# A planned two-layer decoder trunk: half-array products grouped, look-ahead limits per stage, norm weights loaded at first use, large buffers in sets of 18 and 6

## The chip, the cores and the metric

The kernel runs on one core of one Trainium2 chip. The metric is the device time of one execution in microseconds (us), smaller being better. The profile names the engines of the core: PE (TensorE; matrix products, and PEld for its weight loads), DVE (VectorE), ACT (ScalarE), POOL (GpSimd) and SP (SyncE, whose instructions start the DMA transfers).

## The reference

Two layers act on x of 512 positions by 1024 features, in float32. Cut to what matters here:

```python
for i in range(2):
    h = rmsnorm(x, mix_pre_g[i])
    z = h @ w_in[i]                       # 1024 -> 3206 columns, split among three mixers
    out_a = gelu(a_u) * (causal(sgu_w) @ rmsnorm(gelu(a_v)) + sgu_b)   # 4 groups x 64, chunks of 128
    out_b = silu(r_g) * rmsnorm(retention(rotary(r_q), rotary(r_k), r_v))   # 6 heads x 64, chunkwise
    out_c = softmax(f_q @ f_k.T / 8 + c_i - c_j, causal) @ f_v         # 6 heads x 64, c = cumsum(log_sigmoid(f_f))
    x = x + rmsnorm(concat(out_a, out_b, out_c) @ w_o[i], mix_post_g[i])

    h = rmsnorm(x, ffn_pre_g[i])
    g = causal_dwconv3(h @ w_gate[i])     # 1024 -> 4096
    x = x + rmsnorm((gelu(g) * (h @ w_up[i])) @ w_down[i], ffn_post_g[i])

    gate = sigmoid(rmsnorm(x, ple_pre_g[i]) @ w_ple_gate[i])
    x = x + rmsnorm((p[i] @ w_ple_proj[i]) * gate, ple_post_g[i])
```

## The kernel before

**How the work is tiled.** Activations lie with features on the 128 partitions (`hT`, `cc`), four chunks of 128 positions side by side. The large products don't run in plain float32: each operand is split into a high and a low part of the type float32r (`split`, L587: a copy on ACT, a subtraction on DVE), and a product is three float32r products (high by high, high by low, low by high; `mm3`). The names to know are `thl` and `fhl` (split weights), `traw`, `fraw` and `graw` (weights as they come from DRAM), `hT` and `cc` (split activations), `wg`, `wsa`, `wsb` and `wu` (the weights of an FFN block), and `gain` (the weight vectors of the norm before and of the norm after, broadcast over the partitions).

**Half-array products.** Attention and retention run in plain float32, two heads of 64 at a time, and most of their products use 64 rows or 64 columns of the array: in `fox_attend` (L904) the scores `sps` (64 rows, one product for each of two heads and each chunk `c`, of 128, 256, 384 and 512 columns) and the outputs `ops` (64 columns, eight products); in `ret_core` (L959) `ips`, `kvps` and `rops`; in `gating` (L810) four full products, also named `sps`; in `fox_values` (L849) four `cumps`. In the profile a plain float32 product has two records, a float32r product one. A page of the profile that says x14 for `ops` thus speaks of seven products.

**The stages of a layer**, with the stretches of the profiled execution for the first and the second layer: the start (0 to 54, with the first norm and the gating projection); projections and mixers (`mixers`, L777; 54 to 230, and 850 to 1026); the output projection, the embedding product and the entry to the FFN (`out_proj`, L1044; `embed`, L1224; `Seven`, L640, which makes the seven operands of a fast matrix product; 230 to 340, and 1026 to 1135); the steady FFN (`gate_up`, L1082, 32 blocks, with the pieces of `down`, L1133, between them; 340 to 740, and 1135 to 1535); the end of the FFN and the per-layer-embedding gate (`ple`, L1239; 740 to 850, and 1535 to 1612.5).

In `mixers` the three pairs of attention heads are p0, p1 and p2, and so are those of retention. Each attention pair takes scores (`sps`), a softmax on DVE and ACT (`pe`), transposes on PE (`tps`), and outputs (`ops`). Each retention pair ends with `rops`, an ACT square, a DVE sum, two POOL instructions (`vh`, and `y`, a power), a DVE product (`ro`) and transposes on PE (`cps`). Meanwhile PE can run the projections `rps`, `fps` and `gps` (24 float32r products for a block of 128 columns), and later the output projection `wo`.

**What sets the order.** The whole program is first recorded (`record`, L150: every instruction with its dependencies, its buffers and an estimated cost) and then put in order by a planner (`issue`, L224). It simulates the five engines and always gives a free engine the ready instruction that was recorded first. The order that comes out is fixed for each engine (L410), so an instruction that waits holds up all behind it on its engine. Since all instructions are issued from one place, the profile puts all of them on line 408, and groups are told apart by their tiles.

An instruction that opens a new buffer may be taken ahead of the program's order, but `blocked` (L265) holds it back when the buffer's first use lies more than `AHEAD` = 350 recorded instructions ahead of the oldest unfinished one, or when the buffers in between would run short. There are 24 large buffers of 8 KB per partition in two sets (`SETS`, L59): 15 in set X for float32r tiles, 9 in set W for the FFN block's `wg`, `wsa`, `wsb`; other large tiles (kind None in `b8`, L509) go to whichever set has room. There are 12 work buffers of 512 columns (`wk`) and 8 PSUM banks.

The function `gains` (L542) makes the tile `gain` and starts its two DMAs where it is called in the main loop (L1294 to L1301), ahead of the sub-layer that uses it.

```python
if not slots[tag] or s - front > self.AHEAD or (s > front and live[tag][front:s].max() >= bufs):
    return queue(t)
```

Of the kernel before, what the change touches and what calls it, by code (L numbers as in the profile page):

```python
# [27 lines left out]
F32 = mybir.dt.float32  # L28
# [21 lines left out]
class Plan:  # L50
# [8 lines left out]
    SETS = {"X": 15, "W": 9}  # L59

    AHEAD = 350
# [3 lines left out]
    TABLES = (AF.Exp, AF.Gelu_apprx_tanh, AF.Silu, AF.Sigmoid, AF.Sin)  # L65
    HOP = {"PE": 197, "DVE": 128, "ACT": 131, "POOL": 80, "SP": 0}
    HOP_PE = {"PE": 0, "DVE": 250, "ACT": 270, "POOL": 190, "SP": 100}

    def __init__(self, tc):
# [5 lines left out]
        self.fenced = self.strict = False  # L75
        self.kind = {}
# [73 lines left out]
    def record(self, engine, fn, method, args, kw):  # L150
# [23 lines left out]
        if engine == "PE":  # L174
# [6 lines left out]
            t[6:] = [i]  # L181
        self.ops.append((engine, fn, args, kw, deps, used, self.cost(engine, method, outs, ins, args, kw)))

    def cost(self, engine, method, outs, ins, args, kw):
# [13 lines left out]
        if engine == "PE":  # L198
            if method == "transpose":
                return 108, 0, n  # L200
            dt, rows = kw["lhsT"].dtype, kw["lhsT"].shape[0] / P
            if dt == F32R:
                return 0.4427 * n, 0, n * rows
            half = 0.5 if kw["lhsT"].shape[0] == 64 or kw["lhsT"].shape[-1] == 64 else 1
            return half * max(222, n * 4 / 2.4 + 4) if dt == F32 else max(56, n / 2.4), 0, (2 if dt == F32 else 1) * n * rows
        if engine == "ACT":
            func = ([v for v in args if isinstance(v, AF)] + [None])[0]
            self.table[len(self.ops)] = func if func in self.TABLES else None
            pointers += method == "mul" and isinstance(args[2], bass.AP)
            return (50 if psum else 97) + n / 1.196 + 93 * pointers + 93 * ("accum_out" in kw), 0  # L210
# [11 lines left out]
        return 68 + 62 * bool(pointers) + n / rate, 0  # L222

    def issue(self):  # L224
# [35 lines left out]
        order = []  # L260
        parked = {tag: [] for tag in (*slots, *(f"b8 {k}" for k in (*self.SETS, None)))}
# [3 lines left out]
        def blocked(i):  # L265


            for t in ops[i][5]:
# [93 lines left out]
        while len(order) < n:  # L362
            progress = False
            for e in names:
# [117 lines left out]
def body(ctx, tc, a, out):  # L482
# [59 lines left out]
    def gains(post, pre):  # L542

        t = b8("gain", (2, D))
        for i, src in enumerate((post, pre)):
            if src is not None:
                name, l = src
                SY.dma_start(out=t[:, i, :], in_=a[name][l:l + 1, :].to_broadcast([P, D]))
        return t
# [783 lines left out]
```

## Time and profile before

| What | Value |
|---|---|
| time, median of 3 runs | 1617.17 us (1614.98 to 1617.46) |
| the profiled execution's own time | 1614.3 us |
| its span | 1612.5 us |
| granted TensorE clock over the span | 0.998 |
| DVE, ACT, POOL busy | 77%, 52%, 6% |
| bytes moved by DMA | 197.49 MB, 122 GB/s on average |

The span is the time from the first to the last instruction that the profiler records; the execution's own time has some 2 us around it. In the views quoted below, a row of the timeline gives start, duration, engine, operation, output and inputs, and the count of records that it sums up; in brackets stands how long the engine had been idle before it, and what it waited for. Records overlap at their ends, so the distance from one start to the next is the cost of a group, not its duration. A row of the view of windows gives busy times of PE, PEld, DVE, ACT and POOL in a stretch, then the granted clock, the DMA share and GB/s.

### The profile page before, as it was taken

Reading aid. Unit: us, or ns where it says so; the run is one execution under the profiler, and the core shown is the slowest. Engines: PE = TensorE matmul, PEld = TensorE weight load, DVE = VectorE, ACT = ScalarE, POOL = GpSimd, SP = SyncE. Lnnn points to the kernel's source line nnn. Section 1 sums busy time; section 2 is a strip of 40 time slices with the busy share of each in tenths; the row PEclk is TensorE's granted clock in tenths of the full one; section 3 lists DMA queues with packets and bytes.
Section 4 is the critical chain, followed back from the end, with each engine's and each line's share of the span. In section 5 each row is a group of like instructions: output and inputs, shape, how many; then the busy total and the mean of one; then the engine's idle time right before and its main releaser. Section 6 shows DMA issues by size and latency. Waiting matters only on the chain. (4 is left out here: it accounts for less than half of the span.)

```text
span 1612.5 us, 25222 instructions
## 1 busy us (share of the span) xinstructions
PE 1577.5 (98%) x10034; PEld 1393.0 (86%) x10034; DVE 1240.0 (77%) x2013; ACT 840.5 (52%) x1380; POOL 92.0 (6%) x157
## 2 busy tenths in 40 slices
PE   8999998999999999999999999999999999999998
PEld 6887777999999999998888777789999999999977
DVE  6556759988889889877664658599888888888684
ACT  7335526765555555554552445377555455455452
POOL 1000021000000000002220000200000000000022
PEclk9999999999999999999999999999999999999999
DMA  8231316323423423337534114072233233233551
GB/s 298 89 123 53 126 60 222 131 79 105 128 83 105 130 80 105 131 101 270 180 121 157 53 53 170 29 248 92 80 130 105 81 129 105 85 128 107 185 189 53
DMA packets 63422, 197.49 MB, mean 122 GB/s; under 512 B 7348, under 2 KB 15164, under 8 KB 63304
## 3 DMA queue, kind: packets, MB, share of 16 engines
q1 hardware_dynamic: 63160, 195.81, 35.5%
q8 instruction: 79, 1.29, 0.3%
q14 instruction: 39, 0.32, 0.1%
q10 hardware_dynamic: 144, 0.07, 0.0%
HBM read 178.52 MB, written 17.33 MB: 121 GB/s over the span
## 5 line engine op out<-in xcount | busy, mean ns | idle before, releaser
L408 PE MATMUL dn<-thl,act 128*128 128x512 f32 x1536 | 371.5, 391 | 0.0
L408 PEld LDWEIGHTS dn<-thl,act 128*128 128x128 f32 x1536 | 280.0, 188 | 51.9
L408 PE MATMUL ps<-thl,hT 128*128 128x512 f32 (+3 forms) x984 | 207.6, 369 | 1.8 <-DVE thl L408 1.7
L408 PEld LDWEIGHTS ps<-thl,hT 128*128 128x128 f32 x984 | 177.4, 190 | 24.8 <-DVE thl L408 2.6
L408 DVE TENSOR_TENSOR graw<-graw 128x512 f32<-128x512 f32 x256 | 176.3, 690 | 2.7
L408 DVE TENSOR_TENSOR thl<-traw,thl 128x1024 fp32r<-128x1024 f32 (+2 forms) x120 | 140.8, 1186 | 11.3 <-ACT thl L408 11.0
L408 ACT CAST thl<-traw 128x1024 fp32r<-128x1024 f32 (+2 forms) x120 | 119.5, 1020 | 40.3 <-PE dn L408 27.6
L408 PEld LDWEIGHTS beta<-hb,wg 128*128 128x128 f32 x768 | 97.4, 189 | 9.0 <-DVE wg L408 4.0
L408 PEld LDWEIGHTS beta<-hh,wu 128*128 128x128 f32 x768 | 98.3, 189 | 6.1 <-DVE us L408 1.9
L408 PE MATMUL beta<-hb,wg 128*128 128x256 f32 x768 | 99.8, 278 | 3.6 <-DVE wg L408 3.6
L408 PE MATMUL beta<-hh,wu 128*128 128x256 f32 x768 | 100.7, 281 | 1.5 <-DVE us L408 1.5
L408 PE MATMUL ag<-hb,wg 128*128 128x256 f32 x768 | 100.4, 278 | 0.0
L408 DVE TENSOR_TENSOR wg<-graw,wg 128x1024 fp32r<-128x1024 f32 x64 | 78.3, 1224 | 28.0 <-PE beta L408 17.7
L408 PE MATMUL beta<-hh,wsa 128*128 128x256 f32 x768 | 98.2, 277 | 1.7 <-ACT wsa L408 1.6
L408 DVE TENSOR_TENSOR wsb<-graw,wsb 128x1024 fp32r<-128x1024 f32 x64 | 78.3, 1224 | 27.2 <-PE beta L408 18.2
L408 PE MATMUL ag<-hd,wsa 128*128 128x256 f32 x768 | 98.6, 277 | 0.5 <-DVE gs L408 0.3
L408 DVE SCALAR_TENSOR_TENSOR cv<-gs,cw,cv 128x511 f32<-128x511 f32 (+1 forms) x128 | 95.7, 748 | 3.7 <-ACT cv L408 3.5
L408 PE MATMUL beta<-hh,wsb 128*128 128x256 f32 x768 | 98.2, 277 | 0.0
L408 PE MATMUL ag<-hb,wsb 128*128 128x256 f32 x768 | 97.7, 276 | 0.0
L408 PEld LDWEIGHTS ag<-hb,wg 128*128 128x128 f32 x768 | 94.1, 190 | 0.3
L408 PEld LDWEIGHTS beta<-hh,wsa 128*128 128x128 f32 x768 | 92.2, 188 | 2.2 <-ACT wsa L408 2.1
L408 PEld LDWEIGHTS ag<-hd,wsa 128*128 128x128 f32 x768 | 92.1, 188 | 1.1 <-DVE gs L408 0.9
(193 smaller groups left out, 2609.7 us busy)
## 6 DMA issues: line engine op xcount, KB each, us to landing
graw<-in_w_gu_dram SPq DMA_DIRECT2D x128, 512.0 KB, 5.1
traw<-in_w_dn_dram SPq DMA_DIRECT2D x64, 512.0 KB, 4.9
x<-x SPq DMA_DIRECT2D x40, 512.0 KB, 2.6
fraw<-in_w_fm_dram SPq DMA_DIRECT2D x30, 512.0 KB, 7.6
traw<-in_w_wo_dram SPq DMA_DIRECT2D x16, 512.0 KB, 4.6
traw<-in_w_pg_dram SPq DMA_DIRECT2D x16, 512.0 KB, 10.3
x<-in_x_dram SPq DMA_DIRECT2D x8, 512.0 KB, 6.1
traw<-in_w_uv_dram SPq DMA_DIRECT2D x8, 512.0 KB, 6.6
```

Source lines behind the costliest of these rows:

```text
L408: made = o[1](*[self.map(v) for v in o[2]], **{k: self.map(v) for k, v in o[3].items()})
```

## The change

No instruction of work is added or taken away; instructions are put in another order, and buffers are given out by other rules.

- `plan.together()` marks a group of PE instructions. The first of the group takes over the dependencies and the buffers of all, and the planner issues the rest right behind it (`follows`, `then`). Groups are: the four `sps` of `gating`, the four `cumps`, the two heads' `sps` of each chunk, the eight `ops` of a head pair, the eight `ips`, the six `kvps`, and the eleven `rops`.
- `AHEAD` becomes a table with a limit for each stage. `plan.stage` is set where a stage's code is recorded, and `blocked` counts all the buffers that an instruction needs together.
- The class `Gains` takes the place of `gains`: the tile is made and its DMAs are started where a norm first reads it.
- The 24 large buffers are split 18 to 6 instead of 15 to 9.
- The planner's estimated costs change: a cost of switching between kinds of PE products (`SWITCH`, and 95 into plain float32), more for DVE with `accum_out`, for POOL's power and small instructions, and for ACT on under 64 partitions.

```diff
-    SETS = {"X": 15, "W": 9}
-    AHEAD = 350
+    SETS = {"X": 18, "W": 6}
+    AHEAD = {"mix": 460, "wo": 230, "wo2": 230, "emb": 185, "gu0": 720, "gu": 460, "dn": 245, "end": 770, "pg": 450, "pg2": 120}
+    SWITCH = {"F": 110, "T": 9}
...
+    @contextmanager
+    def together(self):
+        self.group = []
+        yield
+        first, *rest = group = self.group
+        self.group = None
+        for i, j in zip(group, rest):
+            self.ops[j][4].add(i)
+            self.follows[i] = j
+        for j in rest:
+            self.ops[first][4].update(d for d in self.ops[j][4] if d not in group)
+            self.ops[first][5].extend(self.ops[j][5])
...
             if kw.get("op") == ALU.pow:
-                return 300 + 165 * n, 0
-            return 160 if pointers == 0 else 200 + 64 * pointers, 0
+                return 460 + 165 * n, 0
+            return 300, 0
...
-                    if not slots[tag] or s - front > self.AHEAD or (s > front and live[tag][front:s].max() >= bufs):
+                    need[tag] += 1
+                    if len(slots[tag]) < need[tag] or s - front > self.AHEAD[self.stages[i]] or (s > front and live[tag][front:s].max() + need[tag] > bufs):
                         return queue(t)
...
-                    _, i = heapq.heappop(ready[e])
+                    if e == "PE" and then is not None:
+                        i = then
+                        ready[e].remove((i, i))
+                        heapq.heapify(ready[e])
+                    else:
+                        _, i = heapq.heappop(ready[e])
...
-    def gains(post, pre):
-        t = b8("gain", (2, D))
-        for i, src in enumerate((post, pre)):
...
+    class Gains:
+        def __init__(self, post, pre):
+            self.src, self.t = (post, pre), None
+        def __getitem__(self, at):
+            if self.t is None:
+                self.t = b8("gain", (2, D))
...
-                for ps, fs in zip(pss, heads):
-                    T.matmul(ps[:, 0:n], lhsT=q[fs, c * P:n], rhs=k[fs, 0:n], start=True, stop=True)
+                with plan.together():
+                    for ps, fs in zip(pss, heads):
+                        T.matmul(ps[:, 0:n], lhsT=q[fs, c * P:n], rhs=k[fs, 0:n], start=True, stop=True)
```

Three places show how PE's order moves. In these rows xN counts instructions, and the number behind a name tells apart the tiles of one name.

The first is the outputs of the first layer's attention pair p1, in PE's order, about 131 to 142 us in the profile of before. Before:

```order
L408 MATMUL rps<-hT,fhl 128x512 x8
L408 MATMUL ops<-fet,mix_414 64x512
L408 MATMUL rps<-hT,fhl 128x512 x10
L408 MATMUL tps<-k_ident,pe 128x128 x4
L408 MATMUL rps<-hT,fhl 128x512 x5
L408 MATMUL ops<-fet,mix_414 64x512
L408 MATMUL ops<-fet,mix_414 64x384 x2
L408 MATMUL ops<-fet,mix_414 64x256 x2
L408 MATMUL ops<-fet,mix_414 64x128 x2
```

And in the changed kernel, at the same place:

```order
L444 MATMUL tps<-k_ident,pe 128x128 x4
L444 MATMUL rps<-hT,fhl 128x512 x8
L444 MATMUL ops<-fet,mix_413 64x512 x2
L444 MATMUL ops<-fet,mix_413 64x384 x2
L444 MATMUL ops<-fet,mix_413 64x256 x2
L444 MATMUL ops<-fet,mix_413 64x128 x2
L444 MATMUL rps<-hT,fhl 128x512 x23
```

The first `ops` product, which stood alone among the projection's products, has moved down to the other seven.

The second is the end of the first layer's retention, on PE: `rops` of p1, then products of the output projection (`wo`, one name for four PSUM banks), then the transposes `cps` that wait for ACT, DVE and POOL. Before:

```order
L408 MATMUL rops<-mix_184,inn 128x64 x4
L408 MATMUL wo_1776<-thl,cc 128x512 x2
L408 MATMUL wo_1819<-thl,cc 128x512 x3
L408 MATMUL wo_1758<-thl,cc 128x512 x3
L408 MATMUL wo_1776<-thl,cc 128x512 x3
L408 MATMUL wo_1819<-thl,cc 128x512 x3
L408 MATMUL wo_1758<-thl,cc 128x512 x3
L408 MATMUL wo_1776<-thl,cc 128x512 x2
L408 MATMUL cps<-k_ident,ro 128x128 x4
```

And in the changed kernel:

```order
L444 MATMUL rops<-mix_171,inn 128x64 x2
L444 MATMUL wo_1762<-thl,cc 128x512
L444 MATMUL wo_1768<-thl,cc 128x512 x3
L444 MATMUL wo_1785<-thl,cc 128x512 x3
L444 MATMUL wo_1793<-thl,cc 128x512 x3
L444 MATMUL wo_1762<-thl,cc 128x512 x3
L444 MATMUL wo_1768<-thl,cc 128x512 x3
L444 MATMUL wo_1785<-thl,cc 128x512 x3
L444 MATMUL wo_1793<-thl,cc 128x512 x3
L444 MATMUL wo_1762<-thl,cc 128x512 x3
L444 MATMUL wo_1768<-thl,cc 128x512
L444 MATMUL cps<-k_ident,ro 128x128 x4
```

Between `rops` and `cps` there are now 26 products where 19 stood. For p2, a little later, 22 products and four transposes stand where 20 products stood; all four banks of `wo` are now open.

The third is the end of the second layer's FFN on PE: the last pieces of `down` (`dn`), the transposes `hps` of the next norm's operand, and the first products of the gate (`ps<-thl,hT`). Before:

```order
L408 MATMUL hps<-k_ident,h 128x128 x4
L408 MATMUL dn<-thl,act 128x512
L408 MATMUL hps<-k_ident,h 128x128 x4
L408 MATMUL dn<-thl,act 128x512 x23
L408 MATMUL hps<-k_ident,h 128x128 x8
L408 MATMUL dn<-thl,act 128x512
L408 MATMUL ps<-thl,hT 128x512 x24
L408 MATMUL hps<-k_ident,h 128x128 x4
```

And in the changed kernel:

```order
L444 MATMUL hps<-k_ident,h 128x128 x4
L444 MATMUL dn<-thl,act 128x512
L444 MATMUL hps<-k_ident,h 128x128 x4
L444 MATMUL dn<-thl,act 128x512 x19
L444 MATMUL ps<-thl,hT 128x512 x8
L444 MATMUL hps<-k_ident,h 128x128 x8
L444 MATMUL ps<-thl,hT 128x512 x21
L444 MATMUL hps<-k_ident,h 128x128 x4
```

The gate's products now begin ahead of the last eight transposes of a chunk, and the last `dn` product no longer stands between transposes and gate.

Over the whole program, the plain float32 products on PE stand in 39 unbroken runs instead of 62, with the same products in them. In the steady FFN PE's order follows the same pattern in both. At the FFN's entry DVE makes the first block's `wg` some seven rows earlier, and the first `wsa` later in relation to PE's products. On SP's queue the two `gain` loads of `out_proj` now stand behind the loads of `x` instead of ahead of the weights `wo`, those of the FFN's end behind loads of `x`, and those of the gate behind loads of `e` and of the first gate weights.

More of the change, by code (lines that the diff above doesn't have):

```diff
@@ L75, in __init__ @@
         self.fenced = self.strict = False
+        self.group, self.follows = None, {}
+        self.stage, self.stages = "mix", []
         self.kind = {}
@@ L265, in blocked @@
         def blocked(i):
-            for t in ops[i][5]:
+            need = Counter()
+            for t in dict.fromkeys(ops[i][5]):
                 if t not in taken:
@@ L1184, in ffn @@
         pieces(31)()
+        plan.stage = "end"
         us = [wd(7, hf) for hf in range(2)]
@@ L1240, in ple @@
         rs = hT.rs
+        plan.stage = "pg"
         e = Rows(ed[l])
```

121 lines of the change are left out of this document (76 added, 45 removed).

## The prediction

> **What bounds the kernel now.** I read the page's head first, then the windows by stage (columns: stretch, its length, busy time of PE, PEld, DVE, ACT, POOL, granted clock, DMA share, GB/s).
>
> ```profile
> span 1612.5 us, 25222 instructions
> PE 1577.5 (98%) x10034; PEld 1393.0 (86%) x10034; DVE 1240.0 (77%) x2013; ACT 840.5 (52%) x1380; POOL 92.0 (6%) x157
> ...
> 230.00:340.00 110.00, 104.16 (x714) 94.22 (x713) 99.31 (x147) 72.53 (x128) 7.21 (x18) 1.00 0.41 144
> 340.00:740.00 400.00, 400.00 (x2852) 373.58 (x2851) 328.67 (x462) 209.86 (x319) 0.00 (x0) 1.00 0.35 116
> ```
>
> PE is the bound, and in the steady FFN it is busy for 400.00 of 400 us. That stretch, twice, is half of the span, and an order that keeps PE's pattern there can win nothing in it. `out_proj` and the FFN's entry leave PE 5.84 us idle in a layer. What can move is there, in the mixers and at the FFN's end: idle time of PE, and time in which PE counts as busy but its products cost more than they need. The waits of PE show the first kind (columns: total, times, longest).
>
> ```profile
> PE hps L408 <- DVE h L408: 13.3, 12, 7.8
> PE cps L408 <- DVE ro L408: 3.7, 6, 1.1
> PE beta L408 <- DVE wg L408: 3.6, 2, 1.8
> PE beta L408 <- ACT wsa L408: 1.6, 1, 1.6
> PE tps L408 <- DVE pe L408: 1.1, 4, 0.3
> ```
>
> Of these 23.3 us, 7.8 are the start's one wait. The PE time without any wait is 1577.5, so no reordering that leaves product costs alone can go below about 1585 (1577.5 plus that start).
>
> **Part 1: grouped float32 products.** The unit is PE's float32r product of 512 columns:
>
> ```profile
> 766.67 28.60 PE L408 MATMUL ps<-thl,hT 128*128 128x512 f32 x125
> ```
>
> 28.60 / 125 gives 0.228 us each. A lone `ops` product of p1, and the other seven:
>
> ```profile
> 131.63 1.78 PE L408 MATMUL rps<-hT,fhl 128*128 128x512 f32 x7
> 133.35 1.07 PE L408 MATMUL ops<-fet,mix 128*64 128x512 f32 x2
> 134.35 2.57 PE L408 MATMUL rps<-hT,fhl 128*128 128x512 f32 x10
> 136.76 0.60 PE L408 MATMUL tps<-k_ident,pe 128*128 128x128 f32 x4
> ...
> 138.84 2.37 PE L408 MATMUL ops<-fet,mix 128*64 128x512 f32 x14 [0.32 <-ACT fet L408]
> 141.13 1.20 PE L408 MATMUL rps<-hT,fhl 128*128 128x512 f32 x4
> ```
>
> Seven products from 131.63 should end at 133.23; `ops` starts at 133.35, 0.12 later. It takes 1.00 to the next start, and the ten after it reach 136.76, 0.13 over 10 x 0.228. The intruder costs 1.25. The remaining seven take 2.29 (138.84 to 141.13), and of their 512-column products only one was without its partner: two heads write different halves of the array's columns. I take eight together to cost the same 2.29, so the lone one's 1.25 goes. By order there are three such per layer: 3 x 1.25 x 2 = **7.5 us**.
>
> Scores next. First p2's four runs, then p1's last, then p0's whole set:
>
> ```profile
> 172.47 1.56 PE L408 MATMUL sps<-fqk 64*128 64x128 f32 x10
> 173.97 2.14 PE L408 MATMUL rps<-hT,fhl 128*128 128x512 f32 x8
> 176.03 0.91 PE L408 MATMUL sps<-fqk 64*128 64x384 f32 x2
> 176.87 2.81 PE L408 MATMUL rps<-hT,fhl 128*128 128x512 f32 x11
> ...
> 180.76 1.12 PE L408 MATMUL sps<-fqk 64*128 64x512 f32 x2
> 181.82 0.73 PE L408 MATMUL rps<-hT,fhl 128*128 128x512 f32 x2
> ...
> 126.23 1.13 PE L408 MATMUL sps<-fqk 64*128 64x512 f32 x4
> ...
> 97.83 2.43 PE L408 MATMUL sps<-fqk 64*128 64x128 f32 x16
> ```
>
> One 512-column score takes 1.06 (180.76 to 181.82), with a row of 1.12; a pair's row lasts 1.13 (126.23), so the partner is free when it comes next. p2 pays 1.50 + 0.84 + 1.06, and again 1.06 for its other 512 product: 4.46 in four runs. p1 pays 3.40 in three. p0's set in one run is 2.43. After the change every set stands in two or three runs; 0.70 (1.50 less a lone 384's 0.84) + 0.84 + 1.06 = 2.60. With 0.25 for a run (the 0.12 + 0.13 above) p1 wins 0.8, p2 1.86 + 0.25, p0 loses about 0.4: 2.5 a layer, **5.0 us**. Retention's `ips`, `kvps`, `rops` lose about four runs a layer: 8 x 0.25 = **2.0**. Together 14.5. What may hide: nothing, as PE is the bound and these are PE's own times. Bounds: nothing if the lone product's cost comes back inside the group, 18 if all 23 runs that go (62 to 39) save as much as the best.
>
> The Trainium skill ("TensorEngine Tiling (Array Packing)", section Tiling Modes) says that a change of tiling mode drains TensorE, and that different tiles run in parallel. The trace's 0.25 per run and the free partner agree with it. By the drain alone, without the partners, the sum would be 23 x 0.25, an estimate of 5.8 us instead of 14.5.
>
> **Part 2: `cps` behind `wo`.** The chain from `rops` over ACT, POOL and DVE to `cps` is longer than the products laid before it:
>
> ```profile
> 207.06 4.60 PE L408 MATMUL wo<-thl,cc 128*128 128x512 f32 x19
> 212.73 0.66 PE L408 MATMUL cps<-k_ident,ro 128*128 128x128 f32 x4 [1.07 <-DVE ro L408]
> ...
> 218.67 4.81 PE L408 MATMUL wo<-thl,cc 128*128 128x512 f32 x20
> 224.09 0.63 PE L408 MATMUL cps<-k_ident,ro 128*128 128x128 f32 x4 [0.61 <-DVE ro L408]
> ```
>
> 19 x 0.228 ends at 211.39, so 1.34 is lost; 20 end at 223.23: 0.86 lost. The chains last 5.67 and 5.42. With 26 products (5.93) and 22 products with four transposes (22 x 0.228, and 0.4) both are covered, just. That is 2.2 a layer, **4.2** after a little for the second, which misses or makes it by 0.03. The third of the three waits per layer (3.7 / 2 - 1.07 - 0.61 = 0.2; p0) gets 20 products where 22 stood; bounds 0.7 lost and 0.4 won in a layer. The waits of `tps` (1.1 in all) get ten projection products between: **1.0**; p1's `ops` wait of 0.32 in each layer goes too: **0.6**.
>
> **Part 3: the ends of the FFN and the gate.** `hps` waits seven times here; these are the sums for layer 0's end (740 to 850) and layer 1's (1535 on), and one wait of the gate's products for their weights:
>
> ```profile
> PE hps L408 <- DVE h L408: 1.6, 4, 0.8
> PE hps L408 <- DVE h L408: 1.1, 3, 0.4
> ...
> 1558.42 4.97 PE L408 MATMUL ps<-thl,hT 128*128 128x512 f32 x21
> 1565.10 0.97 PE L408 MATMUL ps<-thl,hT 128*128 128x512 f32 x3 [1.72 <-DVE thl L408]
> ```
>
> The 21 products end at 1563.21, so that wait costs 1.89, 0.17 beyond its idle time. With 0.17 for each of the seven, the 2.7 become 3.9. The changed order lays 8 and 21 products between transposes where one stood, and has the gate begin ahead of a chunk's last eight transposes. I take nearly all of 3.9 + 1.9: **5.6**. What is late next is the same chain of the last chunk, with 21 x 0.228 = 4.8 us laid in front of it. Bounds: 0 and 5.8.
>
> **Part 4: `out_proj` and the FFN's entry.** DVE is the busier there (99.31 of 110), and what PE waits for is DVE's and ACT's making of `wg` and `wsa`: 3.6 + 1.6 by the waits above. DVE makes `wg` earlier and `wsa` later; the same work must be through before the same products. I take 0 for it, and 0.8 lost on `hps`, whose chunks then find DVE busy with `wg`. The bounds are 4 won (most of these waits gone) and 4 lost (a stall of 2 us more in each layer at `wsa`).
>
> **Part 5: loads and sets.** `gain` loads late: how long one takes is shown at the start.
>
> ```profile
> 1.24 0.42 SPq L408 DMA_DIRECT2D gain<-in_mix_pre_g_dram  x1
> 7.09 1.29 DVE L408 TENSOR_TENSOR h<-x,gain 128x512 f32<-128x512 f32 x2 [7.09 <-DMA gain<-in_mix_pre_g_dram]
> ...
> 196.41 1.77 SPq L408 DMA_DIRECT2D x<-in_x_dram  x4
> ```
>
> It lands in 5.85. In `out_proj` it is issued behind the `x` loads, before at 196 to 198; its first reader comes after the last `wo` product, later than 224.09 above: over 20 us of PE's products hide it. Without that cover a load would cost 5.85. The set W of six holds two blocks of `wg`, `wsa`, `wsb`; the next block's can be written when the block before last is through. PE's pattern in the steady FFN is unchanged, so 0; if each of 60 blocks waited but 0.5 us, 30 would be lost, which nothing in the windows speaks for.
>
> Sum: 14.5 + 4.2 + 1.0 + 0.6 + 5.6 - 0.8 = 25.1, less 0.6 for `cps` of p0, by the nearer half of its bounds in both layers: **24.5**. The profiled execution's 1614.3 becomes 1589.8. The median before, 1617.17, is 2.9 above that execution, so I take 1589.8 + 2.9, rounded to **1592.5**.
>
> **The rivals.**
>
> B. Grouping saves runs and no partner: the group's first waits for all operands, and the eight cost 2.29 + 1.0. Then the 11 of the waits are left: 1606. Against it: the pair at 1.13 against a lone 1.12.
>
> C. The waits come back in other places or a `gain` is late; 9 to 17 less is won: 1600 to 1608. For it: the covers of Part 2 exceed the chains by 0.3 us or less.
>
> D. A stall at the FFN's entry lowers the clock.
>
> ```profile
> 1040.00:1080.00 40.00, 37.01 (x209) 31.64 (x208) 36.19 (x54) 28.05 (x53) 4.24 (x11) 0.96 0.71 241
> ```
>
> Layer 1's entry shows 0.96 in 40 us, 1.6 us lost; with a stall of 4 us at one entry and one more such loss of clock, 1592.5 + 4 + 1.6 = 1598. The Trainium skill ("TensorE: Matmul & The Clock Gate", section Why this matters for your kernels) warns of TensorE gaps over about 3 us, after which it runs at half clock. It speaks against this change, which puts `wsa` later; the waits above reach 1.8 there, and no run here yet shows a longer one.
>
> E. The order does nothing measurable, as DVE's and ACT's chains set the ends: within 3.2 of 1617.
>
> F. Slower: the border between the sets moves the tiles' addresses, and the FFN's products fall into a costlier pairing of operands. Products of one shape do differ:
>
> ```profile
> L408 PE MATMUL dn<-thl,act 128*128 128x512 f32 x1536 | 371.5, 391 | 0.0
> L408 PE MATMUL beta<-hh,wu 128*128 128x256 f32 x768 | 100.7, 281 | 1.5 <-DVE us L408 1.5
> L408 PE MATMUL beta<-hh,wsb 128*128 128x256 f32 x768 | 98.2, 277 | 0.0
> L408 PE MATMUL rps<-hT,fhl 128*128 128x512 f32 x288 | 76.2, 405 | 0.0
> ```
>
> 4 ns (281 - 277) on 4608 FFN products is 18 us, 14 ns (405 - 391) on 1536 `dn` is 21.5: about 40 lost against 24.5 won, 1631. It decides from 25 us, or 4 ns on all 6144. Against it: those tiles lie in both sets as before, and differences of mean durations may come from neighbours.
>
> **How the numbers follow.** Chances: forecast 0.60, B 0.08, C 0.17, D 0.05, E 0.04, F 0.06. The forecast's own bounds: 18 instead of 14.5 and 4 won at the entry give 1585, and the three runs before lie up to 2.5 apart, so 1582; above it lie the lower bounds of Parts 2 to 4 and C up to 1605. The range 1582 to 1605 leaves out B, E, F and C's end, about 2 in 10. A measurement of this kernel can tell about 0.2%, 3.2 us, from no change. Faster by more: forecast, B, C and D, 0.90. Same: E, 0.04. Slower: F, 0.06.
>
> **What would show it.** Right: the eight `ops` of a head pair (x16) and each pair of `sps` (x4) without other products between; `cps` without the waits for `ro`, at most 0.5 in all; `hps` about 11 with the start's 7.8; PE's busy time near 1563; windows of projections and mixers some 10 us shorter each, of the steady FFN still 400 of 400. Wrong: `dn` above 391 ns or `beta` above 281 (F); a DVE wait for `gain` (C); a `wsa` wait above 3 us with a granted clock of 0.9 (D).

## The result and the profile after

| What | Before | After |
|---|---|---|
| median, and the runs' range | 1616.08 us (1614.40 to 1617.46) | 1589.26 us (1587.76 to 1591.39) |
| the profiled execution, and its span | 1614.3, 1612.5 us | 1587.76, 1585.7 us |
| granted clock over the span | 0.998 | 0.996 |

After against before is 0.9838, with a 95% interval of 0.9825 to 0.985: 26.8 us less. The forecast was 1592.5, in 1582 to 1605. Of all the executions below one, of experiment 10, was disturbed (1677.44 us at a granted clock of 0.901) and is left out of its figures.

The head of the page of after, then the rows of the view of waits that belong to PE (awaited by and from whom: total us, times, longest):

```profile
span 1585.7 us, 25202 instructions
PE 1559.8 (98%) x10034; PEld 1388.1 (88%) x10034; DVE 1233.2 (78%) x2013; ACT 837.2 (53%) x1380; POOL 91.3 (6%) x157
```

```profile
PE hps L444 <- DVE h L444: 7.9, 1, 7.9
PE beta L444 <- ACT gs L444: 7.5, 2, 3.8
PE hps L444 <- ACT wg L444: 1.8, 2, 0.9
PE cps L444 <- DVE ro L444: 1.2, 2, 0.7
PE beta L444 <- DVE wsa L444: 0.3, 1, 0.3
```

PE's busy time fell by 17.7 us with the same 10034 records. Its idle time fell by 9.1 (26.8 less 17.7). Of the twelve waits of `hps` for DVE only the start's 7.9 is left, and `cps` waits 1.2 instead of 3.7. Two waits are new: 3.8 us in each layer at the FFN's entry, where `beta`'s first `wsa` product stands, and 0.9 us of `hps` for ACT's `wg`. The waits of `beta` for DVE's `wg` (3.6 in before) are gone.

I cut both traces into stages by the first records of `cumps`, `beta` and `dn` and the last of `beta` in each layer; both layers are added up:

| Stage | Before | After | Won | Predicted |
|---|---|---|---|---|
| start, to the first `cumps` | 61.1 | 60.8 | 0.3 | 0 |
| mixers and `out_proj`, to the first `beta` | 417.6 | 395.8 | 21.8 | 18.9 |
| entry, first `beta` to first `dn` | 104.6 | 105.6 | -1.0 | 0 |
| FFN, to the last `beta` | 814.6 | 813.8 | 0.8 | 0 |
| the FFN's end, the gate and the rest | 214.7 | 209.8 | 4.9 | 5.6 |
| span | 1612.5 | 1585.7 | 26.8 | 24.5 |

What the plain float32 products cost is added up in the way in which the prediction priced them: for each, the distance from its start to the start of PE's next record, without waits, and what the float32r product or transpose just before or just behind a group takes beyond the usual (median) distance of its kind. `ops` went from 22.2 to 14.7 us, the scores of attention from 23.5 to 19.0, retention's products from 28.7 to 25.9. All plain float32 products together went from 79.7 to 64.8.

The PE rows of p1's outputs in after, at the place whose rows the prediction showed:

```profile
131.29 2.09 PE L444 MATMUL rps<-hT,fhl 128*128 128x512 f32 x8
133.31 2.38 PE L444 MATMUL ops<-fet,mix 128*64 128x512 f32 x16
```

All eight stand in one row of 2.38 us, where the seven alone had a row of 2.37: the lone one's time is gone and the eighth rides along.

### The profile page after: what moved, and what is told of

Read it like the earlier page. It is cut to its first block, busy times and chain, and to the rows that moved or that the text cites. A ratio compares the mean times of both kernels' runs of the same rounds, so it can differ in the third digit from the quotient of the medians.

```text
span 1585.7 us, 25202 instructions
## 1 busy us (share of the span) xinstructions
PE 1559.8 (98%) x10034; PEld 1388.1 (88%) x10034; DVE 1233.2 (78%) x2013; ACT 837.2 (53%) x1380; POOL 91.3 (6%) x157
## 4 chain that ended last, share of the span: by engine, by line
PE 95%; DVE 2%; DMA 1%; ACT 1%; POOL 0%; issue 0%; SPq 0%; POOLq 0%; DVEq 0%; ACTq 0%
PE beta L444 22%; PE dn L444 22%; PE ag L444 16%; PE ps L444 15%; PE rps L444 4%; PE fps L444 4%; PE gps L444 2%; PE wo L444 2%; PE sps L444 1%; PE hps L444 1%; PE tps L444 1%; PE ops L444 1%; PE rops L444 1%; DMA graw<-in_w_gu_dram 1%; PE ips L444 0%
## 5 line engine op out<-in xcount | busy, mean ns | idle before, releaser
L444 PE MATMUL dn<-thl,act 128*128 128x512 f32 x1536 | 371.4, 391 | 0.0
L444 DVE TENSOR_TENSOR graw<-graw 128x512 f32<-128x512 f32 x256 | 169.2, 684 | 1.0
L444 PE MATMUL beta<-hh,wsa 128*128 128x256 f32 x768 | 101.4, 281 | 7.8 <-ACT gs L444 7.5
L444 ACT ACTIVATE cv<-gs,cw 128x512 f32<-128x512 f32 x64 | 52.2, 816 | 82.4 <-DVE gs L444 82.4
L444 ACT COPY gs<-beta 128x256 f32<-128x256 f32 x128 | 47.2, 371 | 88.4 <-PE beta L444 86.6
```

Of the source, the lines that this page charges most:

```text
L444: made = o[1](*[self.map(v) for v in o[2]], **{k: self.map(v) for k, v in o[3].items()})
```

## The experiments

Each is the changed kernel with one part undone, or the kernel before with one part alone, unless it says otherwise. Medians stand beside after's 1589.3; the kernel before, run beside each, had medians of 1615.3 to 1615.4.

### 1. The change without its groups

```diff
     def together(self):
-        self.group = []
         yield
-        first, *rest = group = self.group
...
```

> The changed kernel with the grouping taken out (the marks do nothing; limits, norm weights, sets and costs stay). By its order PE has 51 plain float32 runs instead of 39; per layer three scores and one output of a head pair stand without their partner (two of 384 columns, one pair of 512, one ops of 512). Theory A (a lone half-array product costs what a pair costs, and a run 0.25 us): per layer 0.84 + 0.84 + 1.06 + 1.00 + 6 x 0.25 = 5.2, so about 10.5 us over the changed kernel: 1600. Theory B (only the switch of a run counts): 12 x 0.25 = 3 us, 1592. If the order's waits come back as well (tps, ops), 1 to 2 more by either.

Measured: 1599.98 (1597.95 to 1601.75), 0.9904 of before [0.9889, 0.9919]. The plain float32 products cost 76.8 us, 12.0 more than in after: `ops` 18.5, scores 25.0, retention 28.1. The stages agree: mixers and `out_proj` 406.8, eleven more; entries, FFN and ends as in after within 0.4. The groups' worth sits in the products; the whole lost 10.7.

### 2. The groups alone

The kernel after with the limit 350 everywhere, sets of 15 and 9, norm weights loaded early and the old costs, which is before plus the groups:

```diff
-    SETS = {"X": 18, "W": 6}
+    SETS = {"X": 15, "W": 9}
...
-    SWITCH = {"F": 110, "T": 9}
+    SWITCH = {}
```

> The kernel before with the grouping alone (limit 350 everywhere, sets 15 and 9, norm weights early, old costs). 44 plain float32 runs instead of 62, and no half-array product without its partner. Theory A: 14 of the 14.5 us of the grouping are won, about 1602; PE's waits for h, ro, wg and wsa stay as before. Theory B: 18 x 0.25 = 4.5 us, about 1611.

Measured: 1602.77 (1602.16 to 1605.4), 0.9925 [0.991, 0.994]. Plain float32 products 66.3 us. The waits of PE are nearly those of before:

```profile
PE hps L442 <- DVE h L442: 14.0, 13, 7.8
PE cps L442 <- DVE ro L442: 3.8, 4, 1.4
PE beta L442 <- DVE wg L442: 3.5, 2, 1.8
```

The kernel before had 1615.31 beside it, so the groups alone bring 12.5 us; the products' sum is 13.4 lower than before's, and the waits of PE are 20.3 us in all beside 19.7 (the start's left out). From either side, with experiment 1, the groups are worth 10.7 to 12.5 us.

### 3. The eight outputs together, but partners apart

```diff
-                for j in range(NCH):
-                    for s, fs in enumerate(heads):
+                for s, fs in enumerate(heads):
+                    for j in range(NCH):
```

The group stays one run, but now it runs the four products of one head, then the four of the other.

> The changed kernel with the eight ops products of a head pair still in one run, but all four of one head first, then all four of the other, so that neighbours use the same half of the array's columns. Number of runs unchanged, 39. Theory A: partners no longer run side by side, so each of the six sets costs about twice its 2.29 us: 13 us over the changed kernel, about 1602. Theory B (the switch of a run is the price): as the changed kernel, 1589.

Measured: 1602.56 (1601.76 to 1603.5), 0.9921 [0.9906, 0.9935]. PE's rows of p0's outputs; in after the same row is 2.37 long and the next one follows 2.30 behind it:

```profile
112.46 3.93 PE L444 MATMUL ops<-fet,mix 128*64 128x512 f32 x16
116.32 1.89 PE L444 MATMUL fps<-hT,fhl 128*128 128x512 f32 x7
```

From 112.46 to 116.32 is 3.86 us for the same eight products, 1.56 more; over the six sets this is 9.4, and the sum over all `ops` rose by 9.3 (24.0 against 14.7). So what a group of `ops` saves is above all that two heads' products run side by side in the two halves of the array, and not that there are fewer runs. The remaining 4.0 of the 13.3 lost isn't in `ops`: the wait for `gs` at layer 0's entry became 5.7 us long. The planner laid the entry differently: on ACT, three more instructions stand between the cast of `wsa` and the copy `gs`. Why it did so wasn't followed, and I had not expected that part, so it is by luck that the total agrees with theory A's 1602: twice 2.29 was too much.

### 4. Sets of 15 and 9

```diff
-    SETS = {"X": 18, "W": 6}
+    SETS = {"X": 15, "W": 9}
```

> The changed kernel with the large buffers split 15 to 9 as before. Theory: the split itself is worth nothing in the steady FFN (dn 391 ns, beta 276 to 281 ns as in both kernels); by order three more float32 runs, 0.8 us: within 3 us of 1589. Rival F turned round (the border moves the tiles to addresses that pair better): dn or beta differ by some ns and the time by over 10 us. Second rival: with nine buffers in W the first block's wg is made in time, and the stalls of 3.8 us at wsa in each layer go: 1583.

Measured: 1604.30 (1599.38 to 1606.34), 0.9921 [0.9903, 0.9939]. A miss: 15 us lost where at most 3 were expected. The group of the `dn` products, then the waits:

```profile
L444 PE MATMUL dn<-thl,act 128*128 128x512 f32 x1536 | 372.1, 391 | 0.0
```

```profile
PE beta L444 <- ACT gs L444: 7.0, 2, 4.7
PE cps L444 <- DVE ro L444: 4.5, 2, 2.7
PE beta L444 <- ACT wg L444: 2.3, 1, 2.3
```

`dn` has 391 ns on either border (371.4 us in all in after), so the prediction's rival F falls. In the profiled execution (1606.34, the longest of the four) mixers and `out_proj` take 402.2 (6.4 more), entries 113.0 (7.4 more), ends 213.5 (3.7 more), and PE's waits without the start's come to 20.7 us instead of 10.9. The second rival falls too: with nine buffers in W the stall at the entry's `wsa` stayed, 2.3 and 4.7 us.

### 5. One limit of 350 for all stages

```diff
-    AHEAD = {"mix": 460, "wo": 230, "wo2": 230, "emb": 185, "gu0": 720, "gu": 460, "dn": 245, "end": 770, "pg": 450, "pg2": 120}
+    AHEAD = dict.fromkeys(("mix", "wo", "wo2", "emb", "gu0", "gu", "dn", "end", "pg", "pg2"), 350)
```

> The changed kernel with one limit, 350, for all stages (all else as changed). Theory: the limits are what lets the gate and the end of the FFN be prepared ahead, so the waits of hps and of ps for thl at the two ends come back (5.3 us in the decomposition of the traces), and some at the FFN's entry: 1594 to 1600, with the plain float32 products' cost as in the changed kernel. Rival: the limits are worth nothing, as grouping and buffers set the order: 1589.

Measured: 1613.55 (1611.06 to 1616.13), 0.9989 [0.998, 0.9999]. A miss again, and the largest: 24.3 us, nearly all that the change won. PE's waits:

```profile
PE beta L444 <- ACT gs L444: 7.6, 2, 3.8
PE cps L444 <- DVE ro L444: 6.3, 3, 2.5
PE wo L444 <- ACT cc L444: 2.7, 4, 1.2
PE ag L444 <- DVE gs L444: 2.5, 2, 1.3
```

The wait for `gs` stayed; `cps` waits five times as long as in after, and the waits at `wo` and, at the end of the entry, of `ag` are new. Mixers and `out_proj` take 410.4 (14.6 more) and entries 112.6 (7.0 more). The FFN's 819.7 (5.9 more) and the ends' 205.8 (4.0 less) belong together: in each layer ten more products of `dn` come before the last `beta`. Experiment 2 has the same limits with the old sets, loads and costs, and is 10.8 us faster.

### 6. Norm weights loaded early

```diff
     class Gains:
         def __init__(self, post, pre):
             self.src, self.t = (post, pre), None
+            self[:, 0, 0:1]
```

> The changed kernel with the norm weights loaded where they were before (a large buffer and two transfers ahead of out_proj, of the FFN and of the gate). Theory: the late load wins nothing by its transfer, but it frees one of 24 large buffers for tens of us in out_proj and over the whole FFN; one buffer less delays weights: 1590 to 1597. Rival: no difference, 1589.

Measured: 1603.69 (1603.17 to 1604.47), 0.993 [0.9913, 0.9946]: 14.4 lost, the right sign and more than expected. Layer 1's mixers and `out_proj` take 206.2 instead of 197.6, entries 110.4 instead of 105.6. In layer 1 the chain to `cps` is the largest item, ahead of a wait of 2.1 us of `ips`; rows of PE, DVE and POOL there:

```profile
984.58 4.60 PE L444 MATMUL wo<-thl,cc 128*128 128x512 f32 x19 [0.57 <-DVE thl L444]
993.42 0.90 PE L444 MATMUL cps<-k_ident,ro 128*128 128x128 f32 x3 [4.24 <-DVE ro L444]
```

```profile
987.31 3.48 DVE L444 TENSOR_TENSOR thl<-traw,thl 128x1024 fp32r<-128x1024 f32 x3
```

```profile
987.48 3.41 POOL L444 TENSOR_SCALAR vh<-ss 128x8 f32<-128x8 f32 x1 [36.24 <-DVE ss L444]
990.97 1.67 POOL L444 TENSOR_TENSOR y<-vh,minus_half 128x8 f32<-128x8 f32 x1
```

PE waits 4.24 us for a chain in which POOL's instruction `vh` of 8 columns lasts 3.41, as long as the three DVE subtractions beside it. The last section comes back to that.

### 7. The old costs in the planner

```diff
-    SWITCH = {"F": 110, "T": 9}
+    SWITCH = {}
...
-                return 460 + 165 * n, 0
-            return 300, 0
+                return 300 + 165 * n, 0
+            return 160 if pointers == 0 else 200 + 64 * pointers, 0
```

> The changed kernel with the planner's old costs (no cost of a switch, POOL's power at the old price, DVE and ACT as before). Theory: 39 plain float32 runs stay, so their cost stays at 61 us; but cps behind wo is due too early again: its waits for ro rise from 1.2 to about 4, so 1592. By the order, DVE makes the first block's wg and wsa earlier in relation to PE; if that takes the stall of 3.8 us at wsa away in both layers, 1585 instead.

Measured: 1593.77 (1592.31 to 1597.38), 0.987 [0.9855, 0.9885]: 4.5 lost; by the profiled executions, mixers and `out_proj` lose 2.4 and the ends 2.9. The waits of `cps` for `ro` came to 1.0 us, no more than in after. So it isn't POOL's dearer price that makes the planner lay enough products ahead of `cps`, as I had thought, and the wait for `gs` at the entry doesn't come from the prices either: it stayed, at 8.0 in all.

### 8. Groups and sets

Experiment 2 with sets of 18 and 6:

```diff
-    SETS = {"X": 15, "W": 9}
+    SETS = {"X": 18, "W": 6}
```

> The kernel before with the grouping and with sets of 18 and 6, but one limit of 350, early norm weights and old costs. With 15 and 9 the same kernel took 1602.8. Theory (the sets' 15 us, seen when they were taken back, come from float32r weights that can be prepared ahead once X has 18 buffers, whatever the limits): about 1592 to 1597. Rival (the sets pay only with the new limits, which were chosen for them): within 3 of 1602.8.

Measured: 1602.76 (1602.27 to 1603.68), 0.9923 [0.9908, 0.9938]. With the old limits, loads and costs the new border does nothing in sum (1602.77 without it; mixers and `out_proj` 2.3 longer, the ends 2.8 shorter), though taking it out of the whole costs 15.

### 9. A buffer held, with late loads

The changed kernel, with an empty large buffer held for as long as early loads would hold one. It adds two POOL instructions on one column; the loads stay late.

```diff
+            self.hold = b8("hold", (2, D))
+            G.memset(self.hold[:, 0, 0:1], 0.0)
...
+                G.memset(self.hold[:, 0, 0:1], 0.0)
```

> The changed kernel, norm weights loaded late as in it, but one large buffer held empty from where the early loads would have taken it to the first use of the weights (two writes of one column each by POOL). Loading early cost 14.4 us (1603.7). Theory (it is the buffer that the early load keeps from others): most of it comes back, 1599 to 1606, with waits in the same places, the end of layer 1's mixers and the FFN's entries. Rival (it is the place of the two transfers in SP's queue): 1589.

Measured: 1595.78 (1594.64 to 1596.78), 0.9879 [0.9864, 0.9893], in the middle. Entries take 111.5, as in experiment 6 (110.4), but layer 1's mixers and `out_proj` 197.9, as in after (197.6) and not as in experiment 6 (206.2). A held buffer by itself thus costs as much at the entries as the early loads do; what the early loads cost in layer 1's mixers isn't the buffer alone.

### 10. Groups and POOL's price

Experiment 2 with one thing more, POOL's new price:

```diff
-                return 300 + 165 * n, 0
-            return 160 if pointers == 0 else 200 + 64 * pointers, 0
+                return 460 + 165 * n, 0
+            return 300, 0
```

> The kernel before with the grouping and with POOL's new price alone (limit 350, sets 15 and 9, early norm weights, other costs old). Without the price the same kernel took 1602.8, with waits of cps for ro of 3.8 us. By the order 27 products now stand between rops and cps of p1 where 19 stood, and 15 products with six transposes for p2. Theory: the waits for ro fall below 1.5 us and the time by about 3 to 1600. Rival (the wo products that fill the gap are missing later): waits for ro fall, time within 1 of 1602.8.

Measured: 1610.64 (1606.62 to 1612.46), 0.9969 [0.9954, 0.9983]. That is 7.9 slower than experiment 2 and a miss for both sides. The price does what it should, 30 products of `wo` instead of 19 ahead of `cps`, and the chain grew past them:

```profile
201.68 7.09 PE L442 MATMUL wo<-thl,cc 128*128 128x512 f32 x30
210.14 0.65 PE L442 MATMUL cps<-k_ident,ro 128*128 128x128 f32 x4 [1.37 <-DVE ro L442]
```

From the first of the 30 to `cps` it is 8.46 us, where the prediction measured chains of 5.67 and 5.42 in before. But all waits of `cps` for `ro` come to 4.8 us, only 1.0 more than in experiment 2. Most of the loss is elsewhere: mixers and `out_proj`, which reach to the first `beta`, take 414.6 us instead of 404.8, and at that first `beta` PE waits for ACT's `wg`, for which it doesn't wait there in experiment 2.

```profile
PE beta L442 <- ACT wg L442: 7.0, 2, 3.6
```

Why `wg` is that late wasn't followed.

### 11 and 12. Useless products in the entry's idle time

PE is idle 3.77 us at layer 0's entry and runs at half clock behind it. Does the clock cost anything? Both kernels are after with 30 products of 256 columns more, which follow block 0's products of `wg`. In experiment 11 they write the unread half of `beta`'s bank, and there disturb the open sum in the other half for the first block of each layer; in experiment 12 they write the unread half of `ag`'s.

```diff
+            if b == 0:
+                plan.extra[plan.newest] = 30 * [dict(out=ag[:, t2], lhsT=wg[:, 0, 0:P], rhs=h["b11"][:, 0, 0, :], start=True, stop=True, skip_group_check=True)]
```

> The changed kernel with 30 useless float32r products of 256 columns (into a half of a PSUM bank that nothing reads), 3.4 us of PE's time, in each layer's first FFN block between its wg and its wsa products, where PE stands idle for 3.77 us; the order is otherwise the same. Theory (the idle time lowers the clock that is granted right behind it, 0.50 to 0.60 for 3.5 us in layer 0 and 7 us in layer 1): the clock stays at 1.0 there, and 1.7 + 3.4 = 5 us go: 1584. Rival (the low clock comes from something else that happens then, as the burst of loads): the clock falls as before, 1589; if the products delay wsa's, more.

Measured: 1595.17 (1594.57 to 1596.46), 0.9876 [0.9861, 0.9891]. It tells nothing on the clock, since the added products, of line 449, waited themselves for ACT's copy of `beta` and ran behind the stall:

```profile
265.84 5.32 PE L449 MATMUL beta<-hb,wg 128*128 128x256 f32 x30 [3.76 <-ACT gs L444]
```

> As e11_warm, with the 30 useless products written to the unused half of the bank of alpha and gamma, which nobody reads at that time, so that they start right behind wg's products instead of waiting for ACT's copy. They fill 3.4 of the 3.77 us in which PE stood idle. Theory (the idle time lowers the granted clock): the clock stays at 1.0 behind them in both layers, and the 1.7 + 3.4 us lost to it in the changed kernel go: 1584, its entries 50.8 and 49.7 us instead of 52.5 and 53.1. Rival (the low clock comes from something else that happens then): the entries as in the changed kernel, 1589.

Measured: 1586.48 (1585.01 to 1586.98), 0.9815 [0.9801, 0.9828]. Here they fill the stall; rows of PE, then windows (columns as in the prediction) behind the stall in the two layers:

```profile
262.31 3.70 PE L449 MATMUL ag<-hb,wg 128*128 128x256 f32 x30
266.22 0.51 PE L444 MATMUL beta<-hh,wsa 128*128 128x256 f32 x2 [0.21 <-ACT gs L444]
```

```profile
266.00:270.00 4.00, 3.29 (x27) 3.08 (x27) 4.00 (x7) 2.96 (x5) 0.00 (x0) 1.00 1.04 408
1052.00:1056.00 4.00, 4.00 (x37) 4.00 (x37) 4.00 (x6) 2.35 (x5) 0.00 (x0) 1.00 1.02 414
```

And the same windows in after:

```profile
262.00:266.00 4.00, 0.32 (x2) 0.33 (x3) 4.00 (x8) 2.29 (x5) 0.00 (x0) 1.00 1.03 394
266.00:270.00 4.00, 3.71 (x20) 3.41 (x19) 4.00 (x7) 2.23 (x4) 0.00 (x0) 0.57 1.04 420
...
1052.00:1056.00 4.00, 4.00 (x25) 4.00 (x25) 4.00 (x6) 0.82 (x3) 0.00 (x0) 0.64 1.03 417
```

The clock stays at 1.00, so in these two places it was the idle time that lowered it. Yet the entries take 104.0 instead of 105.6, 1.6 us and not 5. One reason is that 1.2 us of the second layer's half clock lie in the idle time itself and cost nothing. Another is that DVE is busy for 4.00 of 4 us in all these windows: PE reaches DVE's `wsa` sooner and waits 0.5 us for it in each layer. The rest shows further on. Up to the first product of `wu` the two entries are 1.2 and 1.9 us shorter than in after; at the first `dn` 0.15 and 1.4 are left, though PE waits for nothing in between. PE rows of layer 0 in after, then in experiment 12:

```profile
299.07 1.52 PE L444 MATMUL beta<-hh,wsb 128*128 128x256 f32 x12
300.43 1.52 PE L444 MATMUL ag<-hb,wsb 128*128 128x256 f32 x12
```

```profile
299.09 1.58 PE L444 MATMUL beta<-hh,wsb 128*128 128x256 f32 x12
300.50 1.58 PE L444 MATMUL ag<-hb,wsb 128*128 128x256 f32 x12
```

The same twelve products take 1.36 us to the next start in after and 1.41 here, at a granted clock of 1.00 in both, and so it is nearly throughout from 282 to 311.8. Why isn't known. This is the lowest median of all kernels run, 2.8 below after's; the two intervals (up to 0.9828, and from 0.9825) overlap, so it isn't shown to be faster.

## Why the prediction was right, and where it wasn't

**What bounds the kernel: right.** PE's 400.00 of 400 us in the steady FFN stayed, and the two FFN stages changed by 0.8 of 814. All else came from the stages named.

**Part 1, grouped products, 14.5: right, mechanism and size.** Measured 14.9 over all plain float32 products: `ops` 7.4 for 7.5, scores 4.6 for 5.0, retention 2.8 for 2.0; `gating`'s four products, which the sum didn't have, changed by 0.1. (1.50 less 0.84 is 0.66 and not 0.70, which would have made the scores' term some 0.2 larger.) Alone on before the groups bring 12.5, and without them the change loses 10.7. By the runs alone the prediction would have had 5.8. Experiment 3 settles it for `ops`: the runs are as few, and yet 9.3 us are lost when partners don't stand next to each other. For the scores and retention it is argued from the rows. Rival B, which gave a group only its saved runs, falls with that.

**Part 2, `cps` and `tps`: `cps` mis-sized.** 4.2 less 0.6, so 3.6, was predicted, and by how much `cps` starts late behind PE's product before it fell from 4.7 to 1.9, so 2.8. The waits of p2 are gone, and so are those of p0, for which 0.6 had been taken off. The step that failed is "both are covered, just": for p1 it is not, and 0.51 and 0.74 us of waiting are left (1.2 in all, where at most 0.5 was to be). The chain there grew from 5.67 to 6.68 us (199.21 to 205.89 in the rows of the last section), past its 26 products of 5.93. What made it longer is DVE's sum `ss`. In before it starts 0.41 us behind the first of the `wo` products (207.06), in after 2.24 us behind it (199.21), since three subtractions stand ahead of it on DVE:

```profile
207.47 0.69 DVE L408 TENSOR_REDUCE ss<-rsq 128x8 f32<-128x512 f32 x1
```

```profile
198.04 3.49 DVE L444 TENSOR_TENSOR thl<-traw,thl 128x1024 fp32r<-128x1024 f32 x3
201.45 0.68 DVE L444 TENSOR_REDUCE ss<-rsq 128x8 f32<-128x512 f32 x1
```

The prediction took the chain's length from before's order, and the changed order changed it. Of `tps`' 1.0, about 0.6 came: the waits themselves (1.1) are gone, but the transposes cost more beside them.

**Part 3, the ends of the FFN and the gate, 5.6: nearly right.** The stage won 4.9. Behind layer 1's last `beta` 3.9 were won (87.12 to 83.22), where the new order stands that the change section shows, and behind layer 0's 1.0 (127.62 to 126.63). In layer 0 four waits of 1.6 in all went, but the transposes `hps` cost 0.5 more there, and one product more falls into the stage.

**Part 4, `out_proj` and entry, 0 and -0.8: two errors that cancel.** The entry got the stall that the bounds named (4 us lost, "a stall of 2 us more in each layer at `wsa`"): 3.77 and 3.75 us with half clock behind. Yet the entries lost only 1.0, because the stall took the place of other waits: within the entry PE waited 4.4 and 2.8 us in before (for `wg`, `wsa`, `us` and `gs`), and 4.1 and 3.8 in after. What I had not put together is the row of DVE at 99.31 of 110. In before the entry takes 52.29 us in the first layer and 52.28 in the second, though only the second has a stretch of half clock: there PE arrives later and waits less for the same results of DVE and ACT (1.65 us for `wsa` become 0.03). In after PE waits for next to nothing behind the stall (0.3 us), so there this is not shown. And `hps`, where 0.8 was to be lost, won: its waits for DVE behind the start's went from 5.5 (13.3 less 7.8; 2.8 of them in `out_proj`) to nothing, with 1.8 new for ACT. Rival D came true as an event, with a clock of 0.50, and not as a price; it gave 1598.

**Part 5, loads and sets, 0: right for what it priced, and silent on what they do.** No `gain` is waited for but the start's, and PE waits for nothing in the FFN. On the groups alone, the sets are worth 0 (experiment 8) and POOL's price costs 7.9 (experiment 10); the limits and the late loads were not tried so. But taken out of the whole, the sets cost 15.0, the late loads 14.4, the limits 24.3, the costs 4.5 and the groups 10.7: 69 us together, where 27 were won. The 13.5 us beyond the groups (1602.8 to 1589.3) belong to no part. They appear when limits, sets and loads come together, and sets, loads and costs without the limits are slower than none of them (experiment 5 against 2). The prediction could name their size only because it read the final order, not the parts.

**What stays open.** Why the planner goes wrong with any one of them undone was followed only in places. A held buffer costs as much at the entries as early loads (experiment 9); a chain to `cps` lengthened by DVE's subtractions makes part of the loss in layer 1's mixers (experiment 6). Why the entry's `wsa` comes late in after can be argued from the trace: DVE runs without a gap there, ACT's cast of `wsa` waits 1.71 us for it, and ACT's copy `gs` stands behind the cast on its queue. The smaller set alone isn't the reason: with nine buffers in it the waits for `gs` were 7.0 us in all (experiment 4), and with six, but the limits, loads and costs of before, 0.9 (experiment 8). Undoing any one part left them at 7.0 to 9.2 (experiments 1 and 4 to 7).

## What to carry to other kernels

Put products that use different halves of the array directly next to each other, and price a lone one at the full pair: that gain held with the other parts and without them. When a new order is to cover a chain, measure the chain again in that order: here it grew along with its cover. The settings of a planner don't add up; take each out of the whole and also set it alone, and let a forecast go by the order that comes out, not by the setting's purpose. Before a wait is priced, look at which engine is busy without a gap on the other side of it: in before, a stretch of half clock in front of a busy DVE left the entry's time where it was (52.29 and 52.28 us).

## What was unexpected of the hardware

**POOL waits for DVE's two-input instructions.** The chain to `cps` in layer 0 of after, by its rows on PE, DVE and POOL:

```profile
199.21 6.17 PE L444 MATMUL wo<-thl,cc 128*128 128x512 f32 x26
205.89 0.66 PE L444 MATMUL cps<-k_ident,ro 128*128 128x128 f32 x4 [0.51 <-DVE ro L444]
```

```profile
202.05 1.22 DVE L444 TENSOR_TENSOR thl<-traw,thl 128x1024 fp32r<-128x1024 f32 x1
```

```profile
202.22 1.14 POOL L444 TENSOR_SCALAR vh<-ss 128x8 f32<-128x8 f32 x1 [38.48 <-DVE ss L444]
203.44 1.67 POOL L444 TENSOR_TENSOR y<-vh,minus_half 128x8 f32<-128x8 f32 x1
...
213.86 0.24 POOL L444 TENSOR_SCALAR vh<-ss 128x8 f32<-128x8 f32 x1 [8.75 <-DVE ss L444]
214.19 2.59 POOL L444 TENSOR_TENSOR y<-vh,minus_half 128x8 f32<-128x8 f32 x1
```

`vh` takes 0.24 us alone and 1.14 beside one DVE subtraction, ending 0.09 behind it (203.36 against 203.27). `y` takes 1.67 or 2.59 in the same way. Those 0.9 us are more than the 0.51 for which `cps` waits here, though the chain of before had them too, and it is `ss` that made it longer. Beside three subtractions in a row `vh` took 3.41 in all five cases of the runs (in experiments 4, 5, 6 and 10). Beside two it took 2.28 in experiments 2 and 8, but 1.14 in before and in experiments 4, 7 and 9:

```profile
208.07 2.35 DVE L408 TENSOR_TENSOR thl<-traw,thl 128x1024 fp32r<-128x1024 f32 x2
```

```profile
208.25 1.14 POOL L408 TENSOR_SCALAR vh<-ss 128x8 f32<-128x8 f32 x1 [41.74 <-DVE ss L408]
```

So it often doesn't get in between them, and at times it does; what decides wasn't followed. The Trainium skill ("SBUF — State Buffer", section SBUF: two separate sides) says that DVE and GpSimd share one port pair, which a DVE instruction with two SBUF inputs holds for its whole length against a GpSimd instruction that reads SBUF. The rows agree, for a single instruction; that the loser can also stay out through two or three in a row is what these runs add.

**Half clock for some 3.4 us at a time.** Windows of 1 us of after (the granted clock is the third number from the end), around the half clock in the first and the second layer:

```profile
266.00:267.00 1.00, 0.97 (x7) 0.68 (x5) 1.00 (x2) 1.00 (x3) 0.00 (x0) 0.70 1.07 414
269.00:270.00 1.00, 1.00 (x7) 1.00 (x7) 1.00 (x3) 0.20 (x1) 0.00 (x0) 0.59 1.02 418
...
1048.00:1049.00 1.00, 0.00 (x0) 0.00 (x0) 1.00 (x3) 1.00 (x2) 0.00 (x0) 0.53 1.01 401
1054.00:1055.00 1.00, 1.00 (x7) 1.00 (x6) 1.00 (x2) 0.00 (x0) 0.00 (x0) 0.56 1.02 418
```

Where the clock is 0.50 inside such a stretch and 1.00 outside, 0.70 and 0.59 put its ends at 266.4 and 269.8, so it lasted 3.4 us; in the second layer it went from 1048.1 to 1054.9, 6.8 us. PE was idle for 3.77 us until 0.7 us before the first stretch, and for 3.75 us until 1.2 us after the start of the second. The Trainium skill ("TensorE: Matmul & The Clock Gate", section What's actually happening) gives half rate after an idle window of about 3.4 us, and after's rows agree. The kernel before, however, at its second layer's entry:

```profile
1068.00 1.65 PE L408 MATMUL beta<-hb,wg 128*128 128x256 f32 x10 [1.78 <-DVE wg L408]
```

```profile
1069.00:1070.00 1.00, 1.00 (x7) 1.00 (x6) 1.00 (x2) 1.00 (x3) 0.00 (x0) 0.51 0.89 344
```

An idle time of 1.78 us was followed by half clock there; at the first layer's entry 1.78 us were followed by 1.00. So the length of one gap alone didn't decide it. The traces' records of the clock show more: in all fourteen, every change of it lies a whole number of 3.413 us behind the first change (in before 309 of them, from 14.31 to 1069.03). Counted in these windows, PE was busy for 0.48 of the one before the half clock of before, from 1065.62 to 1069.03; the first layer's waits of 1.78 and 1.65 us fell into windows busy for 0.52 and 0.53, and the clock stayed. In after the windows before the two stretches were busy for 0.21 and 0.26. Over all fourteen traces, the half clock began only behind windows in which PE was busy for 0.54 or less, and behind every one below 0.47. So a window need not be idle throughout for the clock to be halved behind it, and how the idle time falls on these windows counts, not only how long PE is idle.
